# Attention's row-to-column crossings on ScalarE's DMA queue, pooled products in four banks of the other PSUM pool, the second head's weighting one piece later

## The chip, the cores and the metric

The kernel runs on one core of a Trainium2 chip. The time is device microseconds of one launch. Five engines run their own instruction streams in order: TensorE (PE, with PEld its weight loads), VectorE (DVE), ScalarE (ACT), GpSimd (POOL) and SyncE (SP), which here does nothing but issue DMAs. An instruction that waits on a semaphore holds everything behind it on its engine. Lower is better.

## What is computed

Two layers of a bidirectional encoder over 256 tokens of 1024 channels, in float32. Each layer is a token mixer and a gated MLP, both with a residual; a last RMSNorm follows.

```python
def _token_mixer(xn, ...):
    u, q, k, v, g_pool, g_attn = jnp.split(xn @ w_in, SPLITS, axis=-1)
    # four channel groups: centred mean over 2, 4, 8, 16 tokens, minus the token
    pool_out = einsum('bsgc,gcd->bsgd', pooled, w_pool).reshape(B, S, POOL_WIDTH) * pool_scale
    # three groups of four heads, dilation 1, 4, 16, 129 keys each, T5 bias
    wts = jax.nn.softmax(jnp.stack(lses, axis=0), axis=0)
    attn = jnp.einsum('gbsh,gbshd->bshd', wts, jnp.stack(outs, axis=0))
    merged = sigmoid(g_pool) * (pool_out @ w_a) + sigmoid(g_attn) * (attn_out @ w_b)
    return merged @ w_o

def _conv_ffn(xn, w_up, conv_w, conv_b, w_down):
    a, gval = jnp.split(xn @ w_up, 2, axis=-1)
    a = depthwise_conv3(a, conv_w) + conv_b
    return (jax.nn.gelu(a) * gval) @ w_down
```

## The kernel before

**Products in three parts.** Every weight and every activation is split into a rounded high part and the rest. A product is high times high, high times rest and rest times high, so each weight tile is used by three matmuls. One *piece* of weights is 128 x 1024 numbers, and a piece costs TensorE 12 matmuls of 512 columns, wherever it is used.

**The weight stream.** `Weights` loads raw weights with SP's queue into three buffers (line 145), and splits each piece in two steps: ScalarE casts it to the high part `wh` (line 208), VectorE subtracts to get the rest `wl` (line 210). There are five buffers of split pieces. In the attention stretch a piece is split when the piece four before it is fetched for use, so a cast also needs the buffer that TensorE has just left. A raw buffer is free, and its next load may be issued, once VectorE has made the second `wl` of it. `queue_behind(insts, n)` makes the next n splits stand behind the given instructions in the planner's order.

**The attention stretch.** Between lines 1160 and 1215 the order of PE, ACT and DVE is the order of the source; POOL and SP are placed by the planner. 40 pieces are used there: six blocks of four pieces for queries and keys (n = 0 to 5), eight pieces for the pooled branch's projection, eight for a gate. After each piece `step` runs what the table `steps` lists for it. The table, by the number of the piece that has just been used: 9 and 13 `parts` (splits the keys and queries of the first head group), 17 and 25 `bring`, 21 `scores` 0, 24 `scores` 1, 28 `turn` 0, 29 `weigh` 0 with `scores` 2, 30 `turn` 1, 31 `weigh` 1 with `scores` 3, 36 to 39 `turn` and `weigh` of heads 2 and 3. Each `scores` is followed in the table by its `start_turn`.

**A crossing.** Each of the six blocks leaves rows (tokens on partitions) in `t_ps`, which must become columns. `cross` does it (line 730): VectorE transposes 32 x 32 blocks from PSUM into SBUF, two instructions (line 737); one DMA of 512 KB writes them to DRAM (line 739, on SP's queue); four DMAs of GpSimd's queue read them back, turned (line 744). Crossings 0, 1, 3 and 5 end in the tile `k` (0 and 1 the first group's keys and queries, 3 the keys that `scores` 0 and 1 need, 5 those of 2 and 3). `start_turn` sends the softmax weights of a head the same way: the tiles `turning` and `turned_p`.

**A head.** `scores` makes two banks of logits `s_ps` (lines 1053 and 1059; line 1059 alone reads `k` of the later crossings). For each half VectorE scales and adds the bias (line 1066) and takes the maximum (1072), ScalarE takes the exponential (1075), VectorE inverts the sum and scales (1079, 1080). `turn` splits the returned weights into `pth` (ScalarE, 1098) and `ptl` (VectorE, 1099). `weigh` multiplies them with the values into `o_ps` (1108, 1112); ScalarE and VectorE split the result (1117, 1118).

**The pooled products.** While block n = 1 runs, `pool_out` makes eight products `pool_ps`, two ahead of each piece. Each takes a bank of the pool `mmp`, which has four banks and also holds the two banks of the running block; the pool `acc`, four banks as well, holds nothing then. A bank is free when ScalarE (line 1031) and VectorE (1032) have read it.

**The norm's split.** After each residual sum `to_channels` turns the normalised rows by TensorE, and ScalarE and VectorE split them (lines 507 and 508), in two halves for each half of the tokens. The first product of the next weights (`v_ps`, line 690) needs both parts of the first half.

Of the kernel before, what the change touches and what calls it, by code (L numbers as in the profile page):

```python
# [10 lines left out]
F32 = mybir.dt.float32  # L11
# [6 lines left out]
P = 128  # L18
D = 1024
S = 256  # L20
# [228 lines left out]
def encoder(ctx, tc, x, w_in, w_pool, pool_scale, w_a, w_b, w_o, norm1, norm2, w_up, conv_w,  # L249
            conv_b, w_down, rel_bias, norm_f, onehot, edges, out):  # L250
    nc = tc.nc
# [4 lines left out]
    acc = ctx.enter_context(tc.tile_pool(name="acc", bufs=4, space=bass.MemoryType.PSUM))  # L256
    mmp = ctx.enter_context(tc.tile_pool(name="mmp", bufs=4, space=bass.MemoryType.PSUM))
# [3 lines left out]
    W = Weights(tc, wpool, big)  # L261
# [33 lines left out]
    for l in range(DEPTH):  # L295
        for g in range(NG):
            c0 = C_V + g * 512
            slots = (("m2", 0, 2), ("m2", 1, 2), ("ybig",), ("at2",)) if g == 0 else ()
            for j in range(2):
                tag = "k1" if l == 0 and g == 1 and j == 0 else None  # L300
# [26 lines left out]
        for j in range(2):  # L327
            tag = None if j else "k1"
# [157 lines left out]
    def to_channels(x2, psum, g):  # L486

        tag = "acc" if psum is acc else "mm"  # L490

        def fin(t, r, xn):
            for n in range(4):
                cc = slice(n * 256, (n + 1) * 256)
                nc.vector.scalar_tensor_tensor(
                    out=xn[:, cc], in0=h[:, t, cc], scalar=r[:, 0:1], in1=g[:, cc],
                    op0=ALU.mult, op1=ALU.mult,
                )
            for n in range(2):
                pt = psum.tile([P, 4, P], F32, tag=tag, name="xt_ps")  # L500
                ks = slice(4 * n, 4 * n + 4)
                for k in range(4):
                    c0 = (4 * n + k) * P
                    nc.tensor.transpose(pt[:, k, :], xn[:, c0 : c0 + P], ident)
                oh, ol = (x2[:, ks, part, t, :] for part in (0, 1))
                last = [
                    nc.scalar.copy(out=oh, in_=pt),
                    nc.vector.tensor_sub(out=ol, in0=pt, in1=oh.bitcast(F32)),
                ]
                if n == 0:  # L510
                    yield
            if t == 1:
                W.queue_behind(last, 6)

        return fin
# [37 lines left out]
    def two_sums(x2, nk, *chunks):  # L553

        wide, rests = ([(c, k, kind) for c in chunks for k in range(nk)] for kind in (True, False))  # L560
        first = rests if turns["rest"] else wide
        last = wide if turns["rest"] else rests
        for steps in (first, last):
            for (ps, wh, wl), k, kind in steps:
                out, w, x = (ps, wh, x2[:, k]) if kind else (ps[:, 1], wl, x2[:, k, 0])
                nc.tensor.matmul(  # L566
                    out, w(k), x, start=(steps is first and k == 0),
                    stop=(steps is last and k == nk - 1), skip_group_check=turns["rest"],
                )
        turns["rest"] = not turns["rest"]  # L570
# [21 lines left out]
    def halves(a):  # L592

        return a.rearrange("p (t m) -> p t m", t=2)
# [86 lines left out]
    def v_tile():  # L681
        return acc.tile([P, 512], F32, tag="acc", name="v_ps")
# [12 lines left out]
    def by_tokens(x2, n, at_once=1, then=None, ps=None, begin=0, end=None,  # L695
                  ahead=None):


        if ps is None:
            ps = [mmp.tile([P, 512], F32, tag="mm", name="t_ps") for _ in range(2)]  # L700
        for i0 in range(begin, n if end is None else end, at_once):
            if ahead:
                next(ahead)
            held = [W.get() for _ in range(at_once)]
            for t in range(2):
                for i, piece in enumerate(held, i0):
                    v_sum(ps[t], x2, t, i, piece, n - 1)
            for i, _ in held:
                W.free(i)
            if then:  # L710
                then()
        return ps
# [14 lines left out]
        made = nc.scalar.copy(out=hi, in_=z), nc.vector.tensor_sub(out=lo, in0=z, in1=hi.bitcast(F32))  # L727
        return turned, there, made

    def cross(rows, y, z, name, after=None):  # L730

        with tc.issue_after(after.ins) if after else ExitStack():
            for t in range(2):
                nc.vector.transpose(out=y[:, t].rearrange("p q c j -> p c q j"), in_=rows[t])  # L737
        d = dram.tile([2 * P, 4, P], F32, tag=name, bufs=2, name=name)
        nc.sync.dma_start(
            out=d.rearrange("(t p) q x -> p t (q x)", t=2),  # L740
            in_=y.rearrange("p t q c j -> p t (q c j)"),
        )
        for q in range(4):
            nc.gpsimd.dma_start(  # L744
                out=z[32 * q : 32 * q + 32].rearrange("p a c j -> p a (c j)"),
                in_=d[:, q].rearrange("(a i) x -> i a x", i=32),
            )

    def two_parts(tag, name):


        return big.tile([P, KD, 2, 2, P], F32R, tag=tag, name=name)
# [174 lines left out]
    for l in range(DEPTH):  # L927
# [25 lines left out]
        else:  # L953
            for g in range(NG):
                held = begun[0] if g == 0 else [W.get() for _ in range(4)]
                for t in range(2):
                    if g + t == 0:
                        ps = begun[1]
                    else:
                        ps = v_tile()  # L960
# [56 lines left out]
        def pool_out(po2):  # L1017
            for j in range(2):
                i, (wh, wl) = W.get()
                for gg in range(2):  # L1020
                    for oc in range(2):
                        ps = mmp.tile([P, 2, S], F32, tag="mm", name="pool_ps")
                        cc = slice(oc * P, (oc + 1) * P)
                        two_sums(
                            pooled[2 * j + gg], 2,
                            (ps, lambda k: wh[:, 2 * gg + k, cc], lambda k: wl[:, 2 * gg + k, cc]),
                        )
                        c = 4 * j + 2 * gg + oc
                        sc = hps[:, l, c : c + 1]
                        po = sm.tile([P, 2, P], F32, tag="u", name="po")  # L1030
                        nc.scalar.mul(out=po, in_=halves(ps[:, 1]), mul=sc)
                        nc.vector.scalar_tensor_tensor(  # L1032
                            out=po, in0=halves(ps[:, 0]), scalar=sc, in1=po, op0=ALU.mult, op1=ALU.add
                        )
                        nc.scalar.copy(out=po2[:, c, 0], in_=po)
                        nc.vector.tensor_sub(out=po2[:, c, 1], in0=po, in1=po2[:, c, 0].bitcast(F32))
                    if gg:
                        W.free(i)
                    yield
# [5 lines left out]
        probs, turned, ptiles = {}, {}, {}  # L1045
# [41 lines left out]
        def start_turn(hh):  # L1087
            y = sm.tile([P, 2, 4, 4, 32], F32, tag="gain", bufs=1, name="turning")
            turned[hh] = turned_p[:, hh % 2]
            cross([probs[hh, t] for t in range(2)], y, turned[hh], "turning")  # L1090

        def turn(hh):

# [38 lines left out]
        def bring(half):  # L1132
# [7 lines left out]
            13: ((parts, 1),),  # L1140
            17: ((bring, 0),),
            21: ((scores, 0), (start_turn, 0)),
            24: ((scores, 1), (start_turn, 1)),
            25: ((bring, 1),),
            28: ((turn, 0),),
            29: ((weigh, 0), (scores, 2), (start_turn, 2)),
            30: ((turn, 1),),
            31: ((weigh, 1), (scores, 3), (start_turn, 3)),
            36: ((turn, 2),),
            37: ((weigh, 2),),  # L1150
            38: ((turn, 3),),
# [17 lines left out]
        for n in range(6):  # L1169
            block, which = divmod(n, 2)  # L1170
            if n == 1:
                po2 = two_parts("m2", "po2")
            ps = by_tokens(x2, 4, then=step, ahead=pool_out(po2) if n == 1 else None)
            y = tmp[:, 1].rearrange("p (t q c j) -> p t q c j", t=2, q=4, c=4)
            if n in (2, 4):
                z = tmp[:, 0].rearrange("p (a c j) -> p a c j", a=8, c=4)
            else:

                z = kk[:, (1, 0, None, 0, None, 1)[n]]
            cross(ps, y, z, "crossing")  # L1180
            if n == 1:

                highs = big.tile([P, 2, HPG, 2, P], F32R, tag="xn", name="highs")
                qh, kh = highs[:, 0], highs[:, 1]
                lows = [
                    big.tile([P, 2, 2, 2, P], F32R, tag=f"{tag}0", name="lows") for tag in "qk"
                ]
                turned_p = big.tile([P, 2, 2 * 4, 4, 32], F32, tag="ybig", name="turned_p")
# [4 lines left out]
        for n in range(2):  # L1193
            ps = by_tokens(po2, 4, then=step)
# [27 lines left out]
        for n, cc in enumerate(HALVES):  # L1222
            th = gate("gates")
            ps = by_tokens(at2, 2, 2)
            ks = slice(4 * n, 4 * n + 4)
            y = turned_rows[:, n]
            z = big.tile([P, 2, 4, 4, 32], F32, tag=("q1", "v0")[n], name="merged")
            for t in range(2):

                with tc.issue_after((turning if t else made[1]).ins) if n + t else ExitStack():  # L1230
# [4 lines left out]
                turning, there, made = to_chunks(  # L1235
                    th[:, t], y[:, t], z[:, t], (mh[:, ks, t], ml[:, ks, t])
                )
# [182 lines left out]
```

## Time and profile before

| | |
|---|---|
| three runs | 864.84, 869.8 (median), 871.53 us |
| the profiled run | 873.82 us, of which the span of the profile is 872.0 us |
| granted TensorE clock, mean | 0.997 |
| DVE busy | 664.8 us (76%) |
| POOL busy | 105.9 us (12%) |
| HBM traffic | 178.68 MB read, 19.94 MB written, 228 GB/s over the span |

The span begins with the first instruction of the profile and ends with the last. The rows below are of one profiled execution; each gives the start and the duration in microseconds. In the lists of waits the first number is the idle time in all, the second how often, the third the longest.

### The profile page before, as it was taken

The numbers are of one execution on the slowest core, as the hardware profiler recorded it, in microseconds if no ns is written. First come the engines' busy times: TensorE is split into PE (matmuls) and PEld (weight loads), VectorE is DVE, ScalarE is ACT, GpSimd is POOL, SyncE is SP. The second block draws the span as 40 slices with busy tenths as digits, with TensorE's granted clock in tenths as the row PEclk, the third lists the DMA queues.
The fourth block names the chain that finished last, engine by engine and source line by source line (L and its number), as shares of the span: only waits on it lengthen the run. The fifth ranks groups of instructions, "written<-read, shape, count | busy, mean of one in ns | idle before, by whom it ended". The sixth has DMA issues, their size and how long they took to land.

```text
span 872.0 us, 11540 instructions
## 1 busy us (share of the span) xinstructions
PE 855.1 (98%) x4151; PEld 720.9 (83%) x4151; DVE 664.8 (76%) x1018; ACT 489.8 (56%) x759; POOL 105.9 (12%) x226
## 2 busy tenths in 40 slices
PE   9999998999999999999999999998999999999997
PEld 8888787888888888888888878887888888888886
DVE  6998766777756988888855977587666777987884
ACT  6655543455444766666645555454544555765662
POOL 1801122210011211010000012131100122010100
PEclk9999999999999999999999999999999999999999
DMA  9686897895667978665735578988757398776641
GB/s 320 205 256 207 259 295 240 244 319 172 221 210 247 286 226 240 223 226 189 248 113 193 174 259 276 279 262 260 252 199 267 112 315 274 224 229 214 218 145 50
DMA packets 124418, 199.39 MB, mean 229 GB/s; under 512 B 6904, under 2 KB 69056, under 8 KB 124360
## 3 DMA queue, kind: packets, MB, share of 16 engines
q1 hardware_dynamic: 118056, 181.59, 63.3%
q0 software_dynamic: 6144, 16.79, 7.3%
q8 instruction: 33, 0.54, 0.3%
q10 hardware_dynamic: 160, 0.27, 0.1%
q14 instruction: 25, 0.20, 0.1%
HBM read 178.68 MB, written 19.94 MB: 228 GB/s over the span
## 4 chain that ended last, share of the span: by engine, by line
PE 80%; DMA 8%; DVE 6%; issue 2%; ACT 2%; POOL 1%; POOLq 0%; ACTq 0%; DVEq 0%
PE t_ps L690 31%; PE proj_ps L566 18%; PE v_ps L690 6%; PE res_ps L610 6%; PE res_ps L609 6%; PE res_ps L608 6%; DMA k<-crossing 4%; DMA crossing<-qk_rows 4%; PE v_ps L919 3%; DVE wl L210 2%; PE v_ps L826 1%; POOL k L744 1%; PE o_ps L1112 1%; ACT wh L208 1%; DVE qk_rows L737 1%
## 5 line engine op out<-in xcount | busy, mean ns | idle before, releaser
L210 DVE TENSOR_TENSOR wl<-raw,wh 128x1024 fp32r<-128x1024 f32 x274 | 331.1, 1220 | 110.6 <-ACT wh L208 94.5
L208 ACT CAST wh<-raw 128x1024 fp32r<-128x1024 f32 x274 | 285.4, 1051 | 153.5 <-PE t_ps L690 102.1
L690 PE MATMUL t_ps<-wh,x 128*128 128x512 f32 x960 | 301.6, 391 | 0.0
L690 PEld LDWEIGHTS t_ps<-wh,x 128*128 128x128 f32 x960 | 180.7, 188 | 37.6
L690 PE MATMUL t_ps<-wl,x 128*128 128x512 f32 x480 | 187.0, 390 | 0.0
L566 PE MATMUL proj_ps<-x,wh 128*128 128x512 f32 x448 | 106.5, 390 | 0.0
L690 PEld LDWEIGHTS t_ps<-wl,x 128*128 128x128 f32 x480 | 90.4, 188 | 18.6
L566 PEld LDWEIGHTS proj_ps<-x,wh 128*128 128x128 f32 x448 | 83.1, 188 | 16.6
L608 PE MATMUL res_ps<-wh,actq 128*128 128x512 f32 (+1 forms) x184 | 70.1, 381 | 0.0
L609 PE MATMUL res_ps<-wl,actq 128*128 128x512 f32 (+1 forms) x184 | 70.0, 380 | 0.0
L610 PE MATMUL res_ps<-wh,actk 128*128 128x512 f32 (+1 forms) x184 | 69.9, 380 | 0.0
L566 PEld LDWEIGHTS proj_ps<-x,wl 128*128 128x128 f32 x448 | 56.8, 191 | 2.2 <-DVE a L603 0.5
L566 PE MATMUL proj_ps<-x,wl 128*128 128x256 f32 x448 | 57.7, 283 | 0.0
L690 PE MATMUL t_ps<-wh,po 128*128 128x512 f32 x128 | 40.8, 392 | 0.0
L744 POOL DMA_DIRECT2D k<-crossing x32 | 18.8, 594 | 175.1 <-DVE po L1032 70.9
L610 PEld LDWEIGHTS res_ps<-wh,actk 128*128 128x128 f32 x184 | 34.6, 188 | 6.6
L608 PEld LDWEIGHTS res_ps<-wh,actq 128*128 128x128 f32 x184 | 34.6, 188 | 6.4
L609 PEld LDWEIGHTS res_ps<-wl,actq 128*128 128x128 f32 x184 | 34.6, 188 | 6.3
L744 POOL DMA_DIRECT2D zg<-crossing x32 | 18.5, 585 | 170.2 <-DVE y L1323 49.1
L1075 ACT ACTIVATE p<-s,nm 128x512 f32<-128x512 f32 x16 | 11.6, 725 | 34.7 <-DVE nm L1072 32.7
L477 POOL TENSOR_SCALAR ss<-ss 128x1 f32<-128x1 f32 x8 | 1.8, 223 | 229.6 <-ACT junk L470 229.6
L1319 ACT ACTIVATE y<-a,prm 128x256 f32<-128x256 f32 x44 | 25.3, 597 | 6.7 <-DVE a L603 5.2
(204 smaller groups left out, 1214.0 us busy)
## 6 DMA issues: line engine op xcount, KB each, us to landing
raw<-in_w_up_dram SPq DMA_DIRECT2D x44, 1024.0 KB, 6.2
raw<-in_w_in_dram SPq DMA_DIRECT2D x34, 1024.0 KB, 6.1
raw<-in_w_in_dram SPq DMA_DIRECT2D x50, 512.0 KB, 5.2
raw<-in_w_down_dram SPq DMA_DIRECT2D x22, 1024.0 KB, 5.0
raw<-in_w_a_dram SPq DMA_DIRECT2D x8, 1024.0 KB, 10.1
raw<-in_w_o_dram SPq DMA_DIRECT2D x8, 1024.0 KB, 5.5
crossing<-qk_rows SPq DMA_DIRECT2D x12, 512.0 KB, 4.5
crossing<-crossing SPq DMA_DIRECT2D x12, 512.0 KB, 7.7
```

What stands on the lines that cost most here:

```text
L208: inst = nc.scalar.copy(out=h, in_=src)
L210: inst = nc.vector.tensor_sub(out=l, in0=src, in1=h.bitcast(F32))
L566: nc.tensor.matmul(out, w(k), x, start=(steps is first and k == 0), stop=(steps is last and k == nk - 1), skip_group_check=turns["rest"],)
L608: nc.tensor.matmul(ps, ah, wh, start=first, stop=False, skip_group_check=on)
L609: nc.tensor.matmul(ps, ah, wl, start=False, stop=False, skip_group_check=on)
L610: nc.tensor.matmul(ps, al, wh, start=False, stop=last, skip_group_check=on)
L690: nc.tensor.matmul(ps, x2[:, 2 * n + j, part, t, :], w[:, j, :], start=(n + m == 0), stop=(n == last and m == 5),)
L737: nc.vector.transpose(out=y[:, t].rearrange("p q c j -> p c q j"), in_=rows[t])
L744: nc.gpsimd.dma_start(out=z[32 * q : 32 * q + 32].rearrange("p a c j -> p a (c j)"), in_=d[:, q].rearrange("(a i) x -> i a x", i=32),)
L919: nc.tensor.matmul(ps[t], a[:, k, t, :], w[:, j, :], start=(k + m == 0), stop=(k == KD - 1 and m == 2),)
L1075: nc.scalar.activation(p, s, AF.Exp, bias=nm[:, 0:1], accum_out=z)
L1319: nc.scalar.activation(y, a, AF.Identity, bias=b, scale=w1)
```

## The change

Four edits. `to_channels` puts the next split piece behind the first half's split of the first tokens. The pooled products take their bank from `acc` instead of `mmp`. `cross` takes the queue of its writing DMA as an argument, and both callers in the attention stretch, the six blocks and `start_turn`, give ScalarE's; the MLP's crossings stay on SP's. In the table of steps `turn` 1 moves from piece 30 to 31, `weigh` 1 and the start of head 3's turn from 31 to 32; `scores` 3 stays at 31. Since the order of ScalarE is the order of the source, each writing DMA now stands in ScalarE's stream right behind the splits of its block, or behind the exponentials of its head, and waits there for VectorE's transposes.

```diff
@@ to_channels
                 if n == 0:
+                    if t == 0:
+                        W.queue_behind(last, 1)
                     yield
@@
-    def cross(rows, y, z, name, after=None):
+    def cross(rows, y, z, name, after=None, there=None):
...
-        nc.sync.dma_start(
+        (there or nc.sync).dma_start(
@@ pool_out
-                        ps = mmp.tile([P, 2, S], F32, tag="mm", name="pool_ps")
+                        ps = acc.tile([P, 2, S], F32, tag="acc", name="pool_ps")
@@ start_turn
-            cross([probs[hh, t] for t in range(2)], y, turned[hh], "turning")
+            cross([probs[hh, t] for t in range(2)], y, turned[hh], "turning", there=nc.scalar)
@@ steps
             29: ((weigh, 0), (scores, 2), (start_turn, 2)),
-            30: ((turn, 1),),
-            31: ((weigh, 1), (scores, 3), (start_turn, 3)),
+            31: ((turn, 1), (scores, 3)),
+            32: ((weigh, 1), (start_turn, 3)),
@@ the six blocks
-            cross(ps, y, z, "crossing")
+            cross(ps, y, z, "crossing", there=nc.scalar)
```

In the built program of the changed kernel ScalarE's stream holds twenty DMA issues more, ten a layer, and SP's twenty fewer. From the first head's scores on, ScalarE's order is: two exponentials of head 0, the DMA of `turning` 0, two casts, the DMA of crossing 5, a cast, two exponentials of head 1, the DMA of `turning` 1, a cast, `bring`, two casts, two copies of `pa`, a cast, `pth` 0. VectorE's order up to there is the one of before. In TensorE's stream five matmuls of piece 40 now stand before and between the first two of `weigh` 2. In SP's stream the load of the second norm's gain, which waits until `turning` 3 is written, stands one weight load earlier.

## The prediction

> **What bounds the kernel now.** I read the page's busy times first, then the waits of TensorE, then the timeline of each engine around those waits.
>
> ```profile
> span 872.0 us, 11540 instructions
> PE 855.1 (98%) x4151; PEld 720.9 (83%) x4151; DVE 664.8 (76%) x1018; ACT 489.8 (56%) x759; POOL 105.9 (12%) x226
> ...
> PE s_ps L1059 <- DMA k<-crossing: 6.2, 3, 3.8
> PE o_ps L1108 <- DVE ptl L1099: 1.8, 2, 0.9
> PE pool_ps L566 <- DVE po L1032: 1.2, 4, 0.4
> PE v_ps L690 <- DVE x L508: 0.8, 2, 0.4
> ...
> L210 DVE TENSOR_TENSOR wl<-raw,wh 128x1024 fp32r<-128x1024 f32 x274 | 331.1, 1220 | 110.6 <-ACT wh L208 94.5
> ```
>
> TensorE is busy for 98% and its matmuls are not touched by the change, so all there is to win is its idle time, 872.0 - 855.1 = 16.9 us. The four waits are 6.2 + 1.8 + 1.2 + 0.8 = 10.0 us of it, eleven in number, and each of the four edits is aimed at one of them. After a long wait TensorE also starts slowly:
>
> ```profile
> core 0: us, PE busy (x) PEld busy (x) DVE busy (x) ACT busy (x) POOL busy (x), PEclk, DMA share, GB/s
> 131.20:137.40 6.20, 2.41 (x15) 2.23 (x14) 1.02 (x2) 0.00 (x0) 0.00 (x0) 0.86 0.85 310
> 572.10:573.70 1.60, 1.60 (x17) 1.56 (x15) 1.60 (x3) 0.00 (x0) 0.84 (x2) 1.00 0.77 152
> ```
>
> Both stretches hold one head's scores. The second runs through in 1.60 us; the first has the wait of 3.8 and 2.4 us of work, at a granted clock of 0.86. So that wait cost 0.8 more than its length. With an estimated 0.1 for each of the ten short ones that makes 2 us, and 12.0 us for all eleven.
>
> **The two small edits.** The pooled products (1.2 us): a product waits because its bank is still being read two products later; with four banks of its own it has four products' time, so the wait goes. The norm's split (0.8 us): the `wl` of 1.22 us (L210, page mean) that stands in front of L508 goes behind it; what comes late next is the `wl`, needed only pieces later. Both are taken whole: 2.0 us and their 0.6 of slow starts. If either cover fails, its own wait stays, no more.
>
> **The second head's weighting (1.8 us).** TensorE waits 0.9 us for `ptl` and gets a piece in between, 12 matmuls in 2.7 us (572.10 to 573.70 is scores, then the piece's matmuls follow at 0.227 us apart, as 198.04 to 198.26 below). I take the whole 1.8. But `start_turn` 3 moves a piece too, while `weigh` 3 does not:
>
> ```profile
> 196.41 0.69 DVE L1099 TENSOR_TENSOR ptl<-turned_p,pth 128x512 fp32r<-128x512 f32 x1 [0.86 <-ACT pth L1098]
> ...
> 198.04 0.39 PE L690 MATMUL t_ps<-wh,x 128*128 128x512 f32 x1
> 198.26 0.28 PE L1108 MATMUL o_ps<-pth,vh 128*128 128x256 f32 x1
> ```
>
> Head 3's `ptl` ends at 197.10, 1.2 us before `weigh` 3 begins. Starting 2.7 later it would be 1.5 late in each layer, unless its transfers shorten by that: 0 to 3.0 in all, and I take 0.5, since SP's queue issues nothing there for some microseconds while a load waits for this very transfer.
>
> **The crossings.** A crossing's way in layer 0, and a write that had the DMA engines to itself:
>
> ```profile
> 114.88 0.37 SPq L145 DMA_DIRECT2D raw<-in_w_a_dram  x1
> 116.10 0.37 SPq L739 DMA_DIRECT2D crossing<-qk_rows  x1
> ...
> 142.06 0.37 SPq L739 DMA_DIRECT2D turning<-turning  x1
> ...
> 124.99 2.31 POOL L744 DMA_DIRECT2D k<-crossing  x4 [10.22 <-DMA crossing<-qk_rows]
> ...
> 145.30 2.31 POOL L744 DMA_DIRECT2D turned_p<-turning  x4 [5.55 <-DMA turning<-turning]
> ...
> 135.39 0.91 PE L1059 MATMUL s_ps<-k,q 128*128 128x128 f32 x4 [3.79 <-DMA k<-crossing]
> ...
> 562.65 0.68 PE L1059 MATMUL s_ps<-k,q 128*128 128x128 f32 x4 [0.69 <-DMA k<-crossing]
> ...
> 591.20 0.68 PE L1059 MATMUL s_ps<-k,q 128*128 128x128 f32 x4 [1.66 <-DMA k<-crossing]
> ...
> 114.77 1.31 DVE L737 STREAM_TRANSPOSE qk_rows<-t_ps 128x512 f32<-128x512 f32 x2
> ```
>
> The transposes end at 116.08 and SP issues at 116.10: SP was ready, so a free queue issues nothing earlier. The write then needs 8.9 us (to 124.99) behind a load of twice its size issued 1.2 us before it; alone it needs 3.2 (142.06 to 145.30, same size). On a queue of its own it lies between 3.2 and 8.9. I take 5.0: it shares the engines with that load instead of following it. The gain is 3.9.
>
> [...]
>
> Against it stands ScalarE's own delay. A cast that could start when the block's last matmul leaves a buffer now waits for transposes and issue, 1.31 + 0.39 = 1.7 us:
>
> ```profile
> 868.18 0.39 ACTq L548 DMA_DIRECT2D out_dram<-xn  x1
> ```
>
> The next block's transposes stand behind the `wl` of such casts, so each crossing may be issued up to 1.7 us later (0 at best). I take 1.7, which leaves 2.2 gained per crossing. Of the three waits at scores (3.8, and two in layer 1 of 0.7 and 1.7, which the list adds to 6.2) about 1.6 remains in layer 0 and none in layer 1.
>
> **The wait that is added.** Behind head 0's exponentials ScalarE now waits for `turning`'s transposes, and everything queued there goes late, in a closed loop: casts, their `wl`, crossing 5's transposes behind them, ScalarE's wait for those, a cast, its `wl`, head 1's logits, ScalarE's wait for their transposes, the casts, and last `pth` 0. The rows in layer 1:
>
> ```profile
> 567.59 1.30 DVE L737 STREAM_TRANSPOSE turning<-p 128x512 f32<-128x512 f32 x2
> 568.82 2.32 DVE L210 TENSOR_TENSOR wl<-raw,wh 128x1024 fp32r<-128x1024 f32 x2
> 571.05 1.31 DVE L737 STREAM_TRANSPOSE qk_rows<-t_ps 128x512 f32<-128x512 f32 x2
> 572.28 1.18 DVE L210 TENSOR_TENSOR wl<-raw,wh 128x1024 fp32r<-128x1024 f32 x1
> 573.38 0.68 DVE L1066 SCALAR_TENSOR_TENSOR s<-s_ps,bt 128x512 f32<-128x512 f32 x1
> ...
> 577.65 1.30 DVE L737 STREAM_TRANSPOSE turning<-p 128x512 f32<-128x512 f32 x2
> ...
> 584.89 0.69 DVE L1099 TENSOR_TENSOR ptl<-turned_p,pth 128x512 fp32r<-128x512 f32 x1
> ...
> 566.86 1.99 ACT L208 CAST wh<-raw 128x1024 fp32r<-128x1024 f32 x2
> 569.70 1.06 ACT L208 CAST wh<-raw 128x1024 fp32r<-128x1024 f32 x1 [0.85 <-ACT wh L208]
> ...
> 576.92 1.04 ACT L208 CAST wh<-raw 128x1024 fp32r<-128x1024 f32 x1
> ...
> 582.18 0.59 ACT L1197 COPY pa<-t_ps 128x512 f32<-128x512 f32 x1 [0.77 <-PE t_ps L690]
> ...
> 583.62 0.62 ACT L1098 CAST pth<-turned_p 128x512 fp32r<-128x512 f32 x1
> ...
> 587.54 0.28 PE L1108 MATMUL o_ps<-ptl,vh 128*128 128x256 f32 x1
> ```
>
> Carried through the new order, in this execution's clock: the transposes end at 568.89, with the issue ScalarE is free at 569.3, the two casts start there (566.86 before, 2.4 later); their `wl` start at 570.4 and end at 572.7; crossing 5's transposes end at 574.0 (572.36 before); issue, 574.35; the next cast starts then (569.70 before, 4.65 later); its `wl` at 575.45; head 1's logits at 576.55 (573.38, 3.2 later); `turning` 1 is ready 5.57 after that, as now (573.38 to 578.95), at 582.1; issue, and the cast of 576.92 starts at 582.5, 5.6 later. From there to `pth` it is 6.70 now, of which 0.77 is a wait that is then over: 5.9, so `pth` starts at 588.4 and `ptl`, 1.27 later as now, at 589.7, ends at 590.4. TensorE wants it at 587.54. That is a new wait of 2.8 us at the first head's weighting, in each layer: 5.6. Later steps of the stretch then find TensorE 2.8 later and have room again. The bounds: 0, if ScalarE catches up; 4.6 a layer, if the issue on its queue costs twice 0.39 and a clock loss like the 0.8 follows (2.8 + 1.0 + 0.8).
>
> **The sum.** From the profiled run's 873.8: eleven waits with their slow starts, -12.0; what remains at layer 0's scores, +1.6; the two new waits, +5.6; the last head, +0.5: -4.3, or 869.5. The profiled run is 4.0 above the median of 869.8. Part of that must be the DMA waits that the edit shortens, part may be the profiling; I take half of it off: 867.5.
>
> **Rivals.** *ScalarE catches up.* If its wait holds the casts less than the orders say, the 5.6 falls away: 861.9. For it: ScalarE is idle 44% of the span. Against: the delay runs through a loop in which idle time before a wait cannot be used. It decides below 2.0 us of delay at `pth` 0, for `ptl` has 587.54 - 585.58 to spare. Chance 0.25.
>
> *The write lands no sooner.* The engines were the limit, not the queue; the crossings come 1.7 later for ScalarE's wait and nothing is gained. Then layer 0's scores wait 3.8 + 1.7 and layer 1's 0.7 + 1.7, together 7.9 in place of 1.6, and the last head its 3.0 in place of 0.5: 867.5 + 6.3 + 2.5 = 876.3, slower than 869.8. For it: 310 GB/s at a DMA share of 0.85 in the first window above. Against: the write alone needs a third of its time. It decides at a write of 6.7 us or more, where the 1.7 eats the rest (8.9 - 1.7 = 7.2, less what is lost at the last head). Chance 0.15. [...]
>
> *The change does not do what it says.* The waits at scores are large in this execution alone, and what the other edits win is given back at `weigh` 0: 869.8, no change. For it: the three runs spread over 6.7 us. Chance 0.10.
>
> The forecast, 867.5, has 0.50, with a range of its own of 863 to 872. The range for 8 in 10 is 861 to 875: it takes in most of the first rival and of the second's lower half. One per cent is 8.7 us, about what a measurement of this kernel can tell from no change. Faster than 861.1 needs the first rival and a little more (0.4 of its 0.25, 0.05 of the others, and something for ends that I mis-sized): 0.20. Slower than 878.5 needs the second with the upper bound of the new wait: 0.08. Within: 0.72.
>
> **What would show it.** Right: no wait of `pool_ps` for L1032, of `v_ps` for L508, of the second `o_ps` for `ptl`; waits for `k` of 0 to 2 us; a new wait of `o_ps` for `ptl` or `pth` near 2.8 us, twice; ScalarE idle for VectorE's transposes ahead of casts; a crossing's write in about 5 us. Wrong: no wait at the first weighting (then 862), writes of over 7 us and longer waits for `k` (then 876), or waits of matmuls for `wl`, which I priced at nothing.

## The result, and the profile after

| | before | after |
|---|---|---|
| median | 870.21 us (4 runs, 864.84 to 871.53) | 879.05 us (4 runs, 877.55 to 879.46) |
| profiled run, its span | 873.82, 872.0 us | 879.22, 877.3 us |
| ratio after to before | | 1.011, 95% interval 1.0066 to 1.0155 |

The changed kernel is slower by 9.6 us by the ratio (1.1% of 870), interval 5.7 to 13.5; the medians differ by 8.8. The prediction, 867.5 with a range of 861 to 875, was wrong in sign. All ratios in this document leave out one run, of the kernel `e1_rest`, that took 1435 us at a granted clock of 0.56. The busy times and the waits of TensorE (PE, PEld) and ScalarE (ACT) in the profile after; in a list of waits stand total, number and longest, in microseconds:

```profile
span 877.3 us, 11562 instructions
PE 854.3 (97%) x4151; PEld 721.4 (82%) x4151; DVE 663.5 (76%) x1018; ACT 486.3 (55%) x759; POOL 106.4 (12%) x226
```

```profile
PE s_ps L1061 <- DMA k<-crossing: 11.3, 2, 6.2
...
ACT highs L1131 <- DMA k<-crossing: 9.4, 2, 5.1
...
PE o_ps L1110 <- DVE ptl L1101: 3.3, 4, 1.0
...
PE o_ps L1110 <- ACT pth L1100: 1.4, 2, 0.8
```

TensorE's busy time is as before (855.1); its idle time went from 16.9 to 23.0 us. That is less than the 9.6, in part because the execution profiled before lies 3.6 us above its kernel's median: 1.7 of them are lost before the first crossing (its transposes begin at 75.14, after at 73.44). The waits of `pool_ps` for line 1032, of `v_ps` for `x` and of the second head's `o_ps` for `ptl` are gone, as forecast. ScalarE now waits for the transposes of the blocks (26.8 us) and of `turning` (13.1), also as forecast. But the waits for `k` grew, from three of 6.2 in all to two of 11.3, and the first head's weighting waits in both layers. Around the longest wait TensorE's clock was lower too: from 557 to 572 us, where that wait of 6.19 us stands after, the granted clock was 0.77 after and 1.00 before. In layer 1 the way into the first wait reads so (timeline, after):

```profile
528.92 0.37 ACTq L741 DMA_DIRECT2D crossing<-qk_rows  x1
...
545.25 1.14 ACT L1131 CAST highs<-k 128x512 fp32r<-128x512 f32 x2 [5.13 <-DMA k<-crossing]
...
549.66 1.31 DVE L739 STREAM_TRANSPOSE qk_rows<-t_ps 128x512 f32<-128x512 f32 x2
...
551.00 0.37 ACTq L741 DMA_DIRECT2D crossing<-qk_rows  x1
...
557.33 2.30 POOL L746 DMA_DIRECT2D k<-crossing  x4 [8.50 <-DMA crossing<-qk_rows]
...
567.52 1.19 PE L1061 MATMUL s_ps<-k,q 128*128 128x128 f32 x4 [6.19 <-DMA k<-crossing]
...
594.75 0.38 PE L1110 MATMUL o_ps<-pth,vh 128*128 128x256 f32 x1 [0.62 <-ACT pth L1100]
596.09 0.39 PE L1110 MATMUL o_ps<-ptl,vh 128*128 128x256 f32 x1 [0.96 <-DVE ptl L1101]
```

and the same places before:

```profile
527.47 0.37 SPq L739 DMA_DIRECT2D crossing<-qk_rows  x1
...
540.44 1.14 ACT L1129 CAST highs<-k 128x512 fp32r<-128x512 f32 x2 [2.22 <-DMA k<-crossing]
...
544.85 1.31 DVE L737 STREAM_TRANSPOSE qk_rows<-t_ps 128x512 f32<-128x512 f32 x2
...
546.18 0.37 SPq L739 DMA_DIRECT2D crossing<-qk_rows  x1
...
554.21 2.31 POOL L744 DMA_DIRECT2D k<-crossing  x4 [9.56 <-DMA crossing<-qk_rows]
```

The first row of each is crossing 1's write, the keys of the first head group. (Crossing 0 brings its queries; the text of `e9_first` below has the two exchanged.) From its issue to the cast `highs` that needs it pass 545.25 - 528.92 = 16.3 us after, 13.0 before. In layer 0 it is 15.5 after (96.47 to 111.92) and 13.2 before (97.13 to 110.36). Behind that cast stand ScalarE's casts of the next weights, behind their `wl` the transposes of crossing 3, and so crossing 3 starts 4.8 us later in layer 1 (549.66 against 544.85), 3.4 of it from crossing 1's way, and 1.6 later in layer 0. The same places in layer 0, after (before stands in the prediction):

```profile
117.67 0.37 ACTq L741 DMA_DIRECT2D crossing<-qk_rows  x1
...
123.97 2.30 POOL L746 DMA_DIRECT2D k<-crossing  x4 [7.68 <-DMA crossing<-qk_rows]
...
133.85 1.20 PE L1061 MATMUL s_ps<-k,q 128*128 128x128 f32 x4 [5.08 <-DMA k<-crossing]
```

Crossing 3's way in numbers; TensorE is ready for the scores at their start less their wait:

| crossing 3, us | layer 0 before | after | layer 1 before | after |
|---|---|---|---|---|
| transposes begin | 114.77 | 116.33 | 544.85 | 549.66 |
| write, issue to first read | 8.9 | 6.3 | 8.0 | 6.3 |
| first read to scores | 10.4 | 9.9 | 8.4 | 10.2 |
| scores begin | 135.39 | 133.85 | 562.65 | 567.52 |
| TensorE is ready | 131.60 | 128.77 | 561.96 | 561.33 |

The write did land sooner in the changed kernel. In layer 1 the reads took 1.8 us longer and ate it, so that the whole way is no shorter (17.9 against 17.8); in layer 0 the way shrank by 3.1 us. But against TensorE, which is earlier than before, crossing 3 starts 4.4 us later in layer 0 and 5.4 in layer 1. Less what its way gained, this is what the waits grew by: 1.3 and 5.5 us. So the waits grew by what happened ahead of crossing 3, where the prediction had not looked.

### The profile page after: what moved, and what is told of

The parts are those of the page before. It is cut to its first block, busy times and chain, and to the rows that moved or that the text cites. A ratio compares the mean times of both kernels' runs of the same rounds, so it can differ in the third digit from the quotient of the medians.

```text
span 877.3 us, 11562 instructions
## 1 busy us (share of the span) xinstructions
PE 854.3 (97%) x4151; PEld 721.4 (82%) x4151; DVE 663.5 (76%) x1018; ACT 486.3 (55%) x759; POOL 106.4 (12%) x226
## 5 line engine op out<-in xcount | busy, mean ns | idle before, releaser
L568 PEld LDWEIGHTS proj_ps<-x,wh 128*128 128x128 f32 x448 | 83.2, 188 | 16.5
```

What stands on the lines that cost most here:

```text
L568: nc.tensor.matmul(out, w(k), x, start=(steps is first and k == 0), stop=(steps is last and k == nk - 1), skip_group_check=turns["rest"],)
```

## The experiments

All are edits of the kernel before, and their ratios are to it, with the 95% interval. Microseconds behind a ratio are its share of 870. A profile shows one execution, and not always a typical one: that of `e6_no_wait` took 871.8 us where the kernel's median is 876.1, that of `e10_turn_wait` 874.0 (877.8), that of `e12_even` 870.2 (872.9). In kernels within 1.5 us of the one before, the waits for `k` add up to anything from 1.9 to 6.9. So the lists show where a wait stands, and the ratios what an edit costs.

**Which part of the change.** The four edits were divided in three: the three small ones, the six blocks' writes, the writes of `turning`.

```diff
# e1_rest
                 if n == 0:
+                    if t == 0:
+                        W.queue_behind(last, 1)
                     yield
...
-                        ps = mmp.tile([P, 2, S], F32, tag="mm", name="pool_ps")
+                        ps = acc.tile([P, 2, S], F32, tag="acc", name="pool_ps")
...
-            30: ((turn, 1),),
-            31: ((weigh, 1), (scores, 3), (start_turn, 3)),
+            31: ((turn, 1), (scores, 3)),
+            32: ((weigh, 1), (start_turn, 3)),
# e2_blocks; e4_both has this line and e3's
-            cross(ps, y, z, "crossing")
+            cross(ps, y, z, "crossing", there=nc.scalar)
# e3_turning
-            cross([probs[hh, t] for t in range(2)], y, turned[hh], "turning")
+            cross([probs[hh, t] for t in range(2)], y, turned[hh], "turning", there=nc.scalar)
```

> The kernel before with the norm's split, the pooled products' banks and the later second weighting; every crossing's write stays on SP's queue. Theory 1 (the loss of the change is the writes on ScalarE's queue, the other three edits win what was forecast): the waits for pool_ps 1.2, v_ps 0.8 and the second ptl 1.8 us go with about 1 us of slow starts, the last head costs 0.5: about 4 us faster than before, some 866. Theory 2 (the later second weighting costs at the last head, or what is won ahead of the scores is only waited out there): between 0 and 2 us slower than before.

> The kernel before with the writes of the six blocks' crossings on ScalarE's queue and nothing else. Theory 1 (a write lands no sooner there, and ScalarE's wait for the transposes makes the next ones late): TensorE's waits for k grow from about 6 to 10 or more us, 3 to 7 us slower than before. Theory of the prediction (the write shares the engines with the load ahead of it): a write of crossing 3 lands about 5 us after its issue, the waits for k fall to about 1.6, 4 us faster. Theory 3 (the softmax weights' writes on that queue carry all of the loss): no difference beyond 1 us.

> The kernel before with the writes of the four heads' softmax weights on ScalarE's queue and nothing else. Theory 1: ScalarE's casts behind head 0's exponentials start about 2.4 us later and those behind head 1's up to 5.6; the first head's weighting waits up to 2.8 us in each layer, the waits for k stay: 2 to 6 us slower than before. Theory 3 (these writes carry all of the loss): 9 to 13 us slower. If neither the loop nor the queue matters here: within 1 us of before.

> The kernel before with all ten writes of a layer on ScalarE's queue and nothing else. If the parts add up: the measured 8.8 us of the whole change plus what the other three edits win, 9 to 13 us slower than before, and close to the sum of the two kernels that move one kind of write. If the three other edits win nothing: 8 to 9 us slower.

| kernel | ratio | interval | us |
|---|---|---|---|
| three small edits | 1.000 | 0.9975 to 1.0024 | 0 |
| six blocks' writes | 1.0078 | 1.0042 to 1.0114 | +6.8 |
| `turning`'s writes | 1.0092 | 1.0060 to 1.0125 | +8.0 |
| both kinds of writes | 1.0176 | 1.0144 to 1.0207 | +15.3 |

The two kinds of writes add up (6.8 + 8.0 = 14.8); 15.3 is more than the 9 to 13 expected of both. As both kinds lose, the theory that one of them carries all of the loss falls, and so does the prediction's own of a gain of 4 us by the blocks. The three small edits alone won nothing of the 4 us that theory 1 gave them and lost nothing (2 us either way is within the interval); beside the writes they seem to win 5.7 (15.3 for both, 9.6 for the whole change), a difference known to some 5 us only. What each kind of write does to TensorE, first the blocks' alone, then `turning`'s alone:

```profile
PE s_ps L1059 <- DMA k<-crossing: 9.6, 2, 4.9
```

```profile
PE s_ps L1059 <- DMA k<-crossing: 5.9, 4, 3.1
...
PE o_ps L1108 <- DVE ptl L1099: 3.8, 4, 1.0
PE o_ps L1108 <- ACT pth L1098: 2.7, 2, 1.3
```

The blocks lengthen the waits for `k`; `turning` leaves them alone and makes the weightings late, of the first head and the second (timeline of the same kernel, layer 1):

```profile
591.68 0.39 PE L1108 MATMUL o_ps<-ptl,vh 128*128 128x256 f32 x1 [0.96 <-DVE ptl L1099]
...
602.45 0.38 PE L1108 MATMUL o_ps<-pth,vh 128*128 128x256 f32 x1 [1.33 <-ACT pth L1098]
```

In the two stretches of the weightings (154 to 181 and 582 to 610 us) the granted clock was 0.94 in this execution; in the same stretches before it was 1.00. The eight matmuls on `turned_p` behind the second head's waits took 1.75 us here (at 604.48) and 1.05 before (at 599.89).

**The six blocks: ScalarE's wait, or the queue?** One kernel keeps the wait and leaves the writes on SP's queue; the other moves the writes and takes the wait away, by emitting each behind the first cast of the next block.

```diff
# e5_wait, in cross, for the six blocks
+        if wait:
+            seen = sm.tile([P, 1], F32, tag="rz", name="seen")
+            nc.scalar.copy(out=seen, in_=y[:, 1, 0, 0, 0:1])
         d = dram.tile([2 * P, 4, P], F32, tag=name, bufs=2, name=name)
# e6_no_wait: cross only notes the write (there=nc.scalar), step sends it
+    send_later = 0
...
         def step():
+            for w in list(waiting):
+                if w[0] == 0:
+                    waiting.remove(w)
+                    send(*w[1])
+                else:
+                    w[0] -= 1
             for f, hh in steps.pop(next(places), ()):
```

> The kernel before, its writes all on SP's queue; ScalarE copies one column of each block's transposed rows, and so waits for the transposes where the changed kernel issues the DMA, six times a layer. Theory 1a (ScalarE's wait makes the loss of the blocks' writes): 4 to 7 us slower than before, as the kernel that moves the blocks' writes. Theory 1b (the queue makes it, or SP's loads that pass the write): within 1.5 us of before.

> The kernel before with the six blocks' writes on ScalarE's queue, each one cast later in ScalarE's order, where the transposes are nearly over, so that ScalarE waits some 0.1 us and the issue is as early as on SP's queue. Theory 1a (the wait): within 1.5 us of before. Theory 1b (the queue, or the loads that pass): 4 to 7 us slower. Theory of the prediction (the write shares with the load ahead of it): with its bunching gone, 3 to 4 us faster.

The wait alone: 0.9993 (0.9962 to 1.0025). The queue without most of the wait: 1.0056 (1.0026 to 1.0087), +4.9 us. ScalarE's and TensorE's waits, first with the wait alone, then with the queue:

```profile
ACT seen L740 <- DVE qk_rows L737: 34.1, 12, 3.7
...
PE s_ps L1062 <- DMA k<-crossing: 1.9, 2, 1.4
```

```profile
ACT highs L1137 <- DMA k<-crossing: 9.2, 2, 4.9
ACT wh L208 <- DVE qk_rows L737: 9.0, 4, 2.5
...
PE s_ps L1067 <- DMA k<-crossing: 6.1, 2, 3.5
```

34 us of waiting on ScalarE cost nothing that can be measured: theory 1a falls. 1b stands: it is the queue. ScalarE's wait for crossing 1 (`highs`) is 9.2 here, as in the changed kernel (9.4), though this execution took only 2 us longer than the kernel before. One flaw: here crossing 0's write goes out some 3 us late, behind the pooled products; those of crossings 1 to 5 are on time.

**What the queue does to a write.** The disputed cost by itself:

> Not the encoder: only DMAs of the sizes of the crossings, in trials one after the other, each twice. A trial issues up to two weight loads of 1 MB on SP's queue, then, once VectorE has made two transposes (some 1.3 us), a write of 512 KB on the queue of SP, of ScalarE or of GpSimd, then up to two loads more, and GpSimd's four turned reads of what was written. What is computed is left out; the output is a part of x. Theory 1 (the engines serve what was issued first, whichever queue it is in): the write lands as late on ScalarE's queue as on SP's, within 0.5 us: about 3.2 us with nothing ahead, 5 to 6 behind one load, 8 to 9 behind two; loads issued behind it do not delay it. Theory of the prediction (queues share): behind one load about 5 on SP's and 3.5 to 4.5 on ScalarE's, behind two hardly more, and loads issued behind the write delay it by 1 us or more on ScalarE's queue.

The DMA issues of that program: KB, and the median time from issue to landing, over two trials each. The first letter of a name is the queue of the write (s for SP's, a for ScalarE's, p for GpSimd's), the digits are the loads of 1 MB issued ahead of the write and behind it; `_d` is the write, `_z` the reads, `_lda` the first load. This is one execution of the program.

```profile
s1x_lda<-in_w_a_dram SPq DMA_DIRECT2D x2, 1024.0 KB, 5.7
a1x_lda<-in_w_a_dram SPq DMA_DIRECT2D x2, 1024.0 KB, 5.6
...
s0x_d<-s0x_y SPq DMA_DIRECT2D x2, 512.0 KB, 2.8
...
s1x_d<-s1x_y SPq DMA_DIRECT2D x2, 512.0 KB, 5.9
s1x_z<-s1x_d POOLq DMA_DIRECT2D x8, 128.0 KB, 2.8
a1x_d<-a1x_y ACTq DMA_DIRECT2D x2, 512.0 KB, 5.7
...
s2x_d<-s2x_y SPq DMA_DIRECT2D x2, 512.0 KB, 8.3
...
a2x_d<-a2x_y ACTq DMA_DIRECT2D x2, 512.0 KB, 8.3
...
s11x_d<-s11x_y SPq DMA_DIRECT2D x2, 512.0 KB, 6.0
...
a11x_d<-a11x_y ACTq DMA_DIRECT2D x2, 512.0 KB, 8.0
...
s12x_z<-s12x_d POOLq DMA_DIRECT2D x8, 128.0 KB, 5.5
...
s02x_d<-s02x_y SPq DMA_DIRECT2D x2, 512.0 KB, 3.4
...
a02x_d<-a02x_y ACTq DMA_DIRECT2D x2, 512.0 KB, 3.6
```

Behind one load or two, the write landed as late on ScalarE's queue as on SP's (5.7 and 5.9, 8.3 and 8.3), and a single load ahead as early (5.6 and 5.7): half of theory 1 holds, and of the prediction's sharing with a load ahead, which would have put ScalarE's write at 3.5 to 4.5, this program shows nothing. But with one load ahead, another issued 0.4 us behind the write made it land at 8.0 in place of 5.7 on ScalarE's queue, and at 6.0 in place of 5.9 on SP's, which theory 1 had not expected. On GpSimd's queue a write behind one load took 5.0. With no load ahead, two behind it made no such difference (3.6 and 3.4). So in this program another queue did not bring the write past a load ahead of it, but exposed it to a load behind it, by 2.3 us where there was one ahead as well.

**Which crossing.** One or two writes a layer on ScalarE's queue (`n` is the block):

```diff
-            cross(ps, y, z, "crossing")
+            cross(ps, y, z, "crossing", there=nc.scalar if n == 3 else None)       # e8_third
+            cross(ps, y, z, "crossing", there=nc.scalar if n == 1 else None)       # e9_first
+            cross(ps, y, z, "crossing", there=nc.scalar if n in (0, 2) else None)  # e12_even
```

> The kernel before with crossing 3's write alone (the keys that the first two heads' scores wait for) on ScalarE's queue, one write a layer. It is the crossing from which the prediction argued: a load of 1 MB stands ahead of it, and no load is issued right behind. Theory 1 (a load ahead goes first in any queue): within 1.5 us of before, its write lands no earlier than 7.5 us after the issue. Theory 2 (in this kernel the write of this one crossing does land sooner, 6.3 us as in the changed kernel, and the loss comes from other crossings): 0 to 3 us faster.

> The kernel before with crossing 1's write alone (the queries of the first head group, for which ScalarE waits before it splits more weights) on ScalarE's queue, one write a layer. Loads are issued within 2 us behind this write. Theory 2 (on SP's queue these loads stand behind the write, on another queue they go along with it and past it): the write lands 6 to 7 us after its issue in place of 5, the read parts 2 to 3 us later, the casts and crossing 3 behind them too: 3 to 6 us slower than before, most of what the six writes cost together. Rival (the loss is spread evenly over the six writes): about 1 us slower.

> The kernel before with the writes of crossings 0 and 2 on ScalarE's queue and nothing else. Crossing 1 alone cost 2.4 us, all six 5 to 7; crossing 3 alone nothing. If the rest of the loss lies ahead of the scores too (loads issued behind these writes delay what is read back, bring and the casts behind it): 2 to 4 us slower. If these two matter to nobody and the rest lies with crossings 4 and 5: within 1.5 us of before.

Crossing 3: 1.0003 (0.9979 to 1.0028); its write lands 7.5 and 9.2 us after its issue, as late as theory 1 says, and the 6.3 of the changed kernel does not come of the queue alone. Crossing 1: 1.0028 (1.0004 to 1.0052), +2.4 us. Crossings 0 and 2: 1.0034 (1.0009 to 1.0060), +3.0. The three ahead of crossing 3 together give 5.4, against 6.8 and 4.9 for all six. With some 2 us of uncertainty in each this decides neither for "most of it is crossing 1" nor for "spread evenly", and crossings 4 and 5 were not moved by themselves. How SP's stream passes a write is seen at crossing 1 in layer 1, before (first fence) and in the changed kernel (second):

```profile
526.25 0.37 SPq L145 DMA_DIRECT2D raw<-in_w_in_dram  x1
527.47 0.37 SPq L739 DMA_DIRECT2D crossing<-qk_rows  x1
527.88 0.47 SPq L145 DMA_DIRECT2D raw<-in_w_in_dram  x1
...
532.48 2.31 POOL L744 DMA_DIRECT2D k<-crossing  x4 [17.91 <-DMA crossing<-qk_rows]
```

```profile
527.69 0.92 SPq L145 DMA_DIRECT2D raw<-in_w_in_dram  x2
...
528.92 0.37 ACTq L741 DMA_DIRECT2D crossing<-qk_rows  x1
...
535.74 2.30 POOL L746 DMA_DIRECT2D k<-crossing  x4 [18.79 <-DMA crossing<-qk_rows]
```

Before, the write in SP's stream holds the second load until it is issued itself. In the changed kernel nothing holds it, both loads go ahead, and the first read of what was written starts 6.8 us after its issue (535.74 - 528.92) in place of 5.0. So did the other program's write land later behind two loads than behind one (8.3 and 5.9). The reads, to the cast `highs`, then take 9.5 us in place of 8.0.

**`turning`: the wait, or the queue?** The same two tests.

```diff
# e10_turn_wait, in cross, for start_turn alone
+        if wait:
+            seen = sm.tile([P, 1], F32, tag="rz", name="seen")
+            nc.scalar.copy(out=seen, in_=y[:, 1, 0, 0, 0:1])
# e13_turn_queue: there=nc.scalar in start_turn alone, and as e6_no_wait, but two steps later
+    send_later = 1
```

> The kernel before, its writes all on SP's queue; ScalarE copies one column of each head's transposed softmax weights, and so waits for these transposes where the changed kernel issues the DMA of turning, four times a layer. Theory A (the new wait of the prediction: the casts behind go late and with them the tiles of the weighting): as the kernel that moves the writes of turning alone, 5 to 9 us slower than before, with waits of the weighting matmuls for pth and ptl of 2 to 4 us a layer. Theory B (for these writes too it is the queue, as with the six blocks): within 1.5 us of before.

> The kernel before with the four writes of turning on ScalarE's queue, each two casts later in ScalarE's order, where VectorE's transposes are over, so that ScalarE does not wait for them. Theory A (the wait alone makes the 8 us): within 2 us of before. Theory B (the queue has a share): 3 to 8 us slower.

The wait alone: 1.0096 (1.0062 to 1.0130), +8.4 us. The queue alone: 0.9994 (0.9968 to 1.0020); its profile has no wait of ScalarE for `turning`. With the wait alone:

```profile
ACT seen L740 <- DVE turning L737: 15.7, 8, 2.0
...
PE o_ps L1111 <- DVE ptl L1102: 3.3, 5, 1.0
...
PE o_ps L1111 <- ACT pth L1101: 2.0, 2, 1.0
```

In layer 1 `seen` ends ScalarE's wait of 1.96 us behind head 0's exponentials, and the casts behind it start at 568.60; in the kernel before they start at 566.86, right behind the exponentials. Theory A stands: here it is the wait, and half as much waiting as at the blocks costs all of the 8 us.

**A version that beats both.** A load ahead made a write on SP's queue land at 5.9 us in place of 2.8 in `m1_queues`, and one behind it there at 6.0 in place of 5.9; so the load is issued behind the write, on SP's own queue:

```diff
# e7_order: around the last piece of each block
+            held_back = n in (0, 1, 2, 3, 4, 5)
...
+                last=W.hold if held_back else None,
...
-            cross(ps, y, z, "crossing")
+            wrote = cross(ps, y, z, "crossing")
+            if held_back:
+                W.release(wrote)
# Weights: hold() stops new loads, release() places those held behind the write
...
+                self.loads_behind[m] = inst
```

> The kernel before, all writes on SP's queue, but the weight load that is issued just ahead of the crossings of blocks 1 and 3 is put behind their write. Theory 1 (a write waits for the load ahead of it in any queue): the write of crossing 3 lands about 3.5 to 4.5 us after its issue in place of 8 to 9, k is ready 3 to 5 us earlier, the waits for k fall from about 6 to 2: 3 to 5 us faster. Rival (the reads lose to that load what the write wins, since they share the engines with it): within 1.5 us of before.

> All writes on SP's queue, the load ahead of the crossings of blocks 1 and 3 put behind their write (0.4 per cent faster by itself), together with the norm's split, the pooled products' banks and the later second weighting. If the waits that these three take away are not simply waited out at the scores once k comes earlier: 4 to 7 us faster than before, 863 to 866. Rival (they net nothing here either, as they did by themselves): about 867, 3 us faster.

> The version that beat both kernels, without the later second weighting: the load ahead of crossings 1 and 3 behind their write, the norm's split and the pooled products' banks. The later weighting took the second ptl's 1.8 us with its slow starts away and showed waits of some 2 us at the last head. If it nets nothing: the same time, 864 to 866. If it won what was forecast for it: 1.5 to 2 us slower than that version.

| kernel | median | ratio | interval |
|---|---|---|---|
| order alone | 867.54 us | 0.9963 | 0.9934 to 0.9991 |
| order, and the three small edits | 864.7 us | 0.9949 | 0.9923 to 0.9974 |
| order, norm and pool edits only | 866.7 us | 0.9958 | 0.9931 to 0.9986 |

The second is the fastest kernel here, 4.4 us under the one before and 14 under the changed one. The code holds loads at all six blocks, but only at crossings 1 and 3 does the trace show a load moved, to 0.5 us behind the write. With the order alone:

```profile
PE s_ps L1075 <- DMA k<-crossing: 2.4, 2, 1.5
```

From the issue of crossing 3's write to the scores pass 14.2 us in layer 0 and 15.7 in layer 1, in place of 19.3 and 16.5. Crossing 1 gains nothing by it: its reads land 12.6 and 13.4 us after the write's issue, before 13.1 and 12.9. ScalarE's wait for crossing 1 is gone from the list all the same, but in its place ScalarE waits 22.1 us for the loads that were held back (0.9 before). The difference between the second and the third kernel, and what the small edits add to the order, lie inside the intervals.

## Why the prediction was wrong

**The step that failed** is the one on the crossings: it let each gain 2.2 us (a write of 5.0 in place of 8.9, less 1.7 of ScalarE's delay) and left 1.6 of 6.2 us at the scores. The waits came out at 11.3. Three things were wrong in it.

- *"It shares the engines with that load instead of following it."* This was the author's assumption: in the profile before ScalarE's queue carried two DMAs in all (0.73 and 868.18), neither of them beside a crossing. No run shows the 5.0 us that was taken for crossing 3's write there. This write took 6.3 us in the changed kernel, so 2.6 and 1.7 us of the 3.9 were won. That its queue won them isn't shown: alone on that queue it took 7.5 and 9.2 us and the time stayed the same, and in `m1_queues` a write behind a load landed as late on either queue (5.7 and 5.9).
- What a write wins was taken to arrive at the scores. In layer 1 the reads lost it again (10.2 us in place of 8.4).
- The step asked only for the loads ahead of crossing 3's write. What SP's stream had held back behind the writes of the crossings before it was not asked for: crossing 1's way grew by 2.2 and 3.4 us, and crossing 3 started 4.4 and 5.4 us later against TensorE, not 1.7. Moved by themselves, crossing 1 cost 2.4 us and crossings 0 and 2 cost 3.0.

**ScalarE's delay at the blocks**, 1.7 us a crossing in the prediction, is nothing that can be measured: 34 us of such waiting left the time where it was, within 3 us. So the rival "the write lands no sooner" had the right sign, from half of the right reason: its 1.7 us of waiting a crossing was free, while the moved writes without most of that wait cost 4.9 us; that loads then went ahead of a write, as seen at crossing 1, it didn't have. It had the chance 0.15 and the time 876.3; its sum leaves out the third wait at scores, the 1.66 us at 591.20.

**The wait that is added** was right in kind: the casts behind the exponentials go late in a closed loop and make the weighting late. Its size was 2.8 us a layer, 5.6 in all. In the changed kernel the first head's weighting waits 1.8 us in layer 0 and 1.6 in layer 1 (0.62 + 0.96), 3.4 in all without the slow starts. Alone the writes of `turning` cost 8.0. In that kernel's profile the waits at weightings grew by 4.7 us, from 1.8 to 6.5: 1.9 of these are the first head's, and 2.8 the second's, which the later second weighting hides in the changed kernel. The clock of 0.94 there may make up the rest.

**The three small edits** took away the waits that they were meant to, yet alone they net 0 where about 4.1 was forecast (3.8 of waits and 0.8 of slow starts, less 0.5 at the last head). ScalarE's wait for crossing 1 doubled, from the kernel before

```profile
ACT highs L1129 <- DMA k<-crossing: 4.7, 2, 2.5
```

to the one with the three edits, and the waits at the scores did not shrink:

```profile
ACT highs L1131 <- DMA k<-crossing: 9.0, 2, 4.7
...
PE s_ps L1061 <- DMA k<-crossing: 6.9, 3, 3.9
```

What is won ahead of the scores seems to be waited out at the crossings; one profile argues this and doesn't show it, and the same profile has 1.2 us of waits in the MLP (`proj_ps`) that the one before has not. "If either cover fails, its own wait stays, no more" left out that a gain ahead of a DMA chain can vanish in the chain's wait.

**The last head** was sized at 0.5 for both layers. In the changed kernel it waits 0.96 us in layer 0 and 0.45 in layer 1, within the bounds given.

**Still open**: why crossings 0 and 2, which TensorE doesn't wait for, cost 3.0 us; their wait was not followed to its end. Nor was it found why crossing 3's write took 6.3 us in the changed kernel and 7.5 to 9.2 alone on that queue (with all six blocks' writes there 8.6 and 7.2 in `e2_blocks`, 6.4 and 6.6 in `e6_no_wait`), nor where the 2 us come from by which crossing 1 was already late against TensorE when it was written (part of them is TensorE's own gain at the pooled products).

## What to carry to other kernels

Before a DMA is moved to another queue, list what its issue holds back on the old one: in layer 1 the next load followed crossing 1's write on SP's queue (527.47, then 527.88); with the write on ScalarE's queue two loads were issued ahead of it (from 527.69, the write at 528.92), and its first read started 6.8 us after its issue in place of 5.0. If a load stands ahead of an urgent write, try the other order in the one queue: with it crossing 3's way to the scores was 14.2 and 15.7 us in place of 19.3 and 16.5, and the kernel 3.2 us faster. Follow a crossing to its last read: in layer 1 crossing 3's write won 1.7 us, its reads took 1.8 longer, and the scores had nothing of it. Price a wait added to a busy engine by what is queued behind it: on ScalarE 34 us of waiting at the blocks cost nothing that can be measured, and 16 us cost 8 where the next tiles of the same chain stood behind.

## What the runs showed of the hardware

All of this is from `m1_queues`. With one load ahead of a write, two more issued behind it on the same queue left the write alone (6.0 us, 5.9 without them). But the turned reads, on GpSimd's queue, then took 5.5 us each in place of 2.8; the two loads, issued right behind the write, took 8.0 and 10.6 us, so they were still on their way when the reads began. And a write on ScalarE's queue, with one load ahead and one behind it on SP's, took 8.0 us, almost as long as behind two loads (8.3).
